# Turning keys by VectorE's block transpose in place of TensorE: half of the cross attention's cached keys, and the first attention's new keys by way of DRAM

## The chip, the cores and the metric

The kernel runs on one core of a Trainium2 chip. The metric is the device time of one execution in microseconds (us). A core has TensorE (PE in the profile, with its weight loads as PEld), VectorE (DVE), ScalarE (ACT), GpSimd (POOL) and SyncE (SP), which here issues the DMAs. Each engine works through its own list of instructions in order, and engines wait for each other by semaphores.

## What is computed

The reference is one step of a streaming encoder of two layers, width 1024, in float32. There are 640 rows: a prompt of 512 frames, and 16 new frames of each of 8 running streams, which have 256 cached frames.

```python
for i in range(DEPTH):                    # 2 layers
    h = rmsnorm(x, g_mix[i])
    o = fox_mixer(h) if i % 2 == 0 else mla_mixer(h)
    x = x + o
    x = x + cross_attn(rmsnorm(x, g_cross[i]), mem_k[i], mem_v[i], w_x_q[i], w_x_o[i])
    x = x + swiglu(rmsnorm(x, g_ffn[i]), w_ffn_gu[i], w_ffn_down[i])

def fox_mixer(h, past):                   # 16 heads of 64
    q, k, v, f_pre, gate = split(h @ w_in)
    k_all = concat([past_k, k])           # k (640 x 1024) is an output too
    s = q @ k_all.T * scale + cumulative log forget bias   # causal
    return (softmax(s) @ v_all * sigmoid(gate)) @ w_out

def cross_attn(h, mk, mv, w_q, w_o):      # 4 heads of 256, 256 memory rows
    q = h @ w_q
    s = q @ mk.T * scale                  # mk: 8 cached streams, 1 prompt
    return (softmax(s) @ mv) @ w_o
```

Scores are sums over the head's dimension, so TensorE wants the keys with that dimension on the partitions. In memory they stand the other way round, a frame to a row, and have to be turned.

## The kernel before

The phases run one after the other: `fox_phase`, `cross_phase(0)`, the feed-forward, the MLA attention, `cross_phase(1)`, the feed-forward. Operands are split into a high and a low part (`whi`/`wlo` of a weight, `hT`, `qT`, `kT` of activations, two buffers each), and a product is three passes of matmuls over them (`PASSES`). `load_w` loads a weight in units of 128 x 1024 elements: a DMA into `raw`, a cast by ACT to `whi` (L150), a subtraction by DVE to `wlo` (L151). The projections' matmuls stand at L204.

`merge` takes lists of steps and interleaves them evenly. A scheduler then fixes from these steps the order of instructions of each engine, so an edit of one list can move the instructions of others. PE works in order, and a matmul that waits holds up all behind it; SP issues nearly all DMAs, in order too.

**The first attention.** Two heads make a pair `pr` (0 to 7), two pairs a group `g` (0 to 3). `k_list(g)` computes 256 columns of new keys, row by row, into `krow` (640 rows as 5 tiles), stores them as outputs, and `tr(j)` turns them for each pair: four PE transposes of the prompt's rows (L539), one of the streams' rows (L543), then `kT` (high by ACT, low by DVE, L222/L223) and `kn` (L544). The cached keys `kr` are brought in pieces of 32 features (L684) and turned by DVE's block transpose (L692). For each pair, `prompt_list(pr)` computes the prompt's attention in three rounds: scores of query tile 3 (L627, 512 columns, 6 matmuls for two heads), the softmax (a reduction by DVE, L634; an exponential by ACT, L637; reciprocal and scaling by DVE, L344 and L345), transposes of the weights on PE (L650) with their copies to `PT` (L655 by DVE, L657 by ACT), then tile 2 (384 columns), their values (L665), and tiles 1 and 0. `sample_list(pr)` does the streams' part (scores L712 with `Qbd` and `KT`). What fills PE between the steps of this chain is `fill`: the projections of the next pair (`q_list`, `k_list`, `v_list`) and the output projection of the pair before.

**The cross attention.** For each of two pairs of heads, two halves of the streams, two heads and four streams, `keys(hh, b)` turns one block of cached keys (256 rows x 256 features) of `kr`: four PE transposes (L956), then one copy to `KT`, by DVE for even `b` (L960), by ACT for odd (L962). There are 32 blocks in a layer, 64 in all. The queries `q_list(h)` take their weights from `w_x_q`.

Of the kernel before, what the change touches and what calls it, by code (L numbers as in the profile page):

```python
# [9 lines left out]
F32 = mybir.dt.float32  # L10
F32R = mybir.dt.float32r
# [7 lines left out]
P = 128  # L19
D = 1024  # L20
KD = D // P
NP = 512
NT = 640
# [69 lines left out]
def fox_mla_kernel(ctx: ExitStack, tc: tile.TileContext, I, O):  # L93
# [42 lines left out]
    def psum_t():  # L136
        return pat.tile([P, 512], F32, tag="t", name="ps_t", bufs=2)
# [267 lines left out]
    def fox_phase():  # L405
# [8 lines left out]
        with ExitStack() as st:  # L414
# [5 lines left out]
            ckd = drp.tile([NH, NP], F32, name="ckd")  # L420
            csd = drp.tile([P, KS], F32, name="csd")
            lfd = drp.tile([P, NH], F32, name="lfd")
            Qbd = [fp.tile([P, B, 32], F32, name=f"Qbd{i}", bufs=1) for i in range(2)]

            def pw_tile():
# [96 lines left out]
            def k_list(g):  # L522
                c0 = 256 * g
                d = {}

                def load():
                    d["w"] = load_w([(0, 256, w_in[:, 1024 + c0:1024 + c0 + 256])])
                    d["row"] = fp.tile([P, TT, 256], F32, tag="krow", name="krow", bufs=1)

                def store():  # L530
                    S.dma_start(ko[:, :, c0:c0 + 256], d["row"][:, 0:TT - 1, :])
                    S.dma_start(kso[:, c0:c0 + 256], d["row"][:, TT - 1, :])

                def tr(j):
                    cs_ = slice(j * P, (j + 1) * P)
# [6 lines left out]
                    pt = psum_t()  # L542
                    T.transpose(out=pt[:, 0:P], in_=d["row"][:, TT - 1, cs_], identity=ident)  # L543
                    V.tensor_copy(kn, pt[:, 0:P])  # L544
                    ks[2 * g + j] = (kT, kn)

                L = [load]
                for t in range(TT):
                    L += gemm(lambda t=t: as_ops(nx.T, slice(t * P, (t + 1) * P), d["w"], slice(0, 256), KD), 256,
                              lambda ps, t=t: A.copy(d["row"][:, t, :], ps[:, 0:256]), parts=2)  # L550
                return L + [store, lambda: tr(0), lambda: tr(1)]

            def q_list(pr):
                c0 = P * pr
# [236 lines left out]
                    nx.all(t + 1)  # L791
                vl[1 + t]()
            vl[-1]()
            merge(logf_list(), k_list(0) + q_list(0))
            mems = mem_list(0, lambda: fp) + mem_list(1, lambda: fp)
            for pr in range(8):
                fill = []
                if pr % 2 == 1 and pr < 7:
                    fill += k_list(pr // 2 + 1)
# [28 lines left out]

    def cross_phase(l, nx, rest):
        w_q, w_o = I["w_x_q"][l], I["w_x_o"][l]  # L830
        mk = I["cache_mem_k"][l].rearrange("b (m p) h d -> p (b m) (h d)", p=P)
        mv = I["cache_mem_v"][l].rearrange("b (m p) h d -> p (b m) (h d)", p=P)
        with tc.tile_pool(name=f"x{l}", bufs=2, reuse_waits="tile") as xp:
            AHEAD = 3
# [5 lines left out]
            def q_list(h):  # L840
                Q = Qps[h // 2]
                L = []
                d = {}

                def load(dt):
                    if dt == 0:
                        qs_[h] = [xp.tile([P, 2, NP], F32R, tag=f"qT{i}", name=f"qT{i}", bufs=2) for i in range(2)]
                    c0 = h * XD + dt * P
                    d[dt] = load_w([(0, P, w_q[:, c0:c0 + P])], per=8)

                def done(ps, dt, half):
                    qT = qs_[h]
                    n = HALF if half == 0 else NP - HALF
                    hs = slice(half * HALF, half * HALF + n)
                    evac_split(qT[0][:, dt, hs], qT[1][:, dt, hs], ps[:, 0:n], X_SCALE)
                    if half == 1:
                        o = TS * (h % 2)
                        A.activation(Q[:, 2 * (h % 2) + dt, :, o:o + TS],
                                     ps[:, n:HALF].rearrange("p (b t) -> p b t", t=TS), AF.Copy, scale=X_SCALE)

                for half in range(2):
                    for dt in range(2):
                        if half == 0:
                            L.append(lambda dt=dt: load(dt))
                        L += gemm(lambda dt=dt, half=half: ws_ops(d[dt], slice(0, P), nx.T,
                                                                  slice(half * HALF, (half + 1) * HALF), KD),
                                  HALF, lambda ps, dt=dt, half=half: done(ps, dt, half), parts=3)
                return L

            def softmax(pw, sp):  # L870
                nm = small.tile([P, 1], F32, tag="nm", name="nm")
# [5 lines left out]
            def prompt_list(h):  # L877
# [57 lines left out]
            def load_key(n):  # L935

                if n < 32:
                    pr, bq, hh, b = n // 16, n // 8 % 2, n // 4 % 2, n % 4
                    hc = slice((2 * pr + hh) * XD, (2 * pr + hh + 1) * XD)
                    krs[n] = xp.tile([P, 2, XD], F32, tag="kr", name="kr", bufs=4)  # L940
                    S.dma_start(krs[n], mk[:, 2 * (4 * bq + b):2 * (4 * bq + b) + 2, hc])

            def sample_list(pr, bq):
                Q = Qps[pr]
# [2 lines left out]
                def keys(hh, b):  # L947
                    n = 16 * pr + 8 * bq + 4 * hh + b
                    load_key(n + AHEAD)
                    kr = krs.pop(n)  # L950
                    if b % 2 == 0:
                        d["KT"][hh, b // 2] = xp.tile([P, 2, 2, NMEM], F32, tag="KT", name="KT", bufs=4)
                    pt = psum_t()
                    for dt in range(2):
                        for mt in range(2):
                            T.transpose(out=pt[:, dt * NMEM + mt * P:dt * NMEM + (mt + 1) * P],  # L956
                                        in_=kr[:, mt, dt * P:(dt + 1) * P], identity=ident)
                    src = pt.rearrange("p (d m) -> p d m", m=NMEM)
# [71 lines left out]
            for n in range(AHEAD):  # L1030
                load_key(n)
            ql = q_list(0)
            for f in ql[:6] + rest[:1] + ql[6:8] + rest[1:] + ql[8:] + q_list(1):
# [761 lines left out]
```

## Time and profile before

| | before |
|---|---|
| median of 3 runs | 2091.75 us (2089.7 to 2093.53) |
| the profiled execution's own time | 2091.71 us |
| its span, first to last instruction | 2089.9 us |
| PE busy | 2034.7 us, 97% |
| DVE busy | 1390.8 us, 67% |
| ACT busy | 888.0 us, 42% |
| granted TensorE clock, mean | 0.996 |
| DMA, mean share of 16 engines | 38.8% |

The time outside the span is 1.8 us. Busy times of matmuls overlap each other, because they are pipelined: a single one shows longer than the distance from its start to the next one's. What a matmul costs PE is therefore read from starts.

### The profile page before, as it was taken

What the parts mean: (1) busy time and instruction counts of PE and PEld (TensorE: products, weight loads), DVE (VectorE), ACT (ScalarE), POOL (GpSimd) and SP (SyncE); (2) the same over time, 40 slices, a digit from 0 to 9 for tenths busy, and PEclk for the clock granted to TensorE, in tenths of its full rate; (3) what the DMA queues carried; (4) which work ended last, traced back from release to release, by engine and by line L of the source; (5) the groups of instructions that cost most, each with busy time, mean ns of one, the idle gap of its engine ahead of it and who ended that gap; (6) DMA issues with size and microseconds to landing.
All of it is one profiled execution on the core that took longest, in us unless ns stands there. A gap on an engine that the chain in (4) does not pass through costs nothing. (4 is left out here: it accounts for less than half of the span.)

```text
span 2089.9 us, 34810 instructions
## 1 busy us (share of the span) xinstructions
PE 2034.7 (97%) x13629; PEld 1817.9 (87%) x13629; DVE 1390.8 (67%) x2658; ACT 888.0 (42%) x1723; POOL 195.2 (9%) x398
## 2 busy tenths in 40 slices
PE   7999999999999999999999989999999999999998
PEld 7988888777987899999998978887987899999996
DVE  5455555655556896687677567777556896686686
ACT  4434444544443443343344455554443443343342
POOL 1222222210000000000002301101000000000000
PEclk9999999999999999999999999999999999999999
DMA  7565655477464322232222342113463322232221
GB/s 194 119 160 124 148 135 142 146 243 229 151 197 133 100 88 74 81 91 71 81 82 64 96 109 52 53 51 102 149 196 131 101 81 75 80 99 71 81 81 61
DMA packets 334203, 236.37 MB, mean 113 GB/s; under 512 B 99140, under 2 KB 298564, under 8 KB 334040
## 3 DMA queue, kind: packets, MB, share of 16 engines
q1 hardware_dynamic: 334040, 234.15, 38.8%
q8 instruction: 108, 1.77, 0.4%
q14 instruction: 55, 0.45, 0.1%
HBM read 216.90 MB, written 17.21 MB: 112 GB/s over the span
## 5 line engine op out<-in xcount | busy, mean ns | idle before, releaser
L204 PE MATMUL mm<-hT,whi 128*128 128x320 f32 x1744 | 287.5, 311 | 2.9 <-ACT hT L222 2.9
L151 DVE TENSOR_TENSOR wlo<-raw,whi 128x1024 fp32r<-128x1024 f32 (+4 forms) x145 | 169.8, 1174 | 156.5 <-ACT whi L150 116.5
L204 PEld LDWEIGHTS mm<-hT,whi 128*128 128x128 f32 x1744 | 261.0, 188 | 6.8 <-ACT hT L222 4.3
L332 DVE TENSOR_TENSOR X<-mm,X 128x512 f32<-128x512 f32 x270 | 183.5, 687 | 119.7 <-PE mm L204 118.1
L150 ACT CAST whi<-raw 128x1024 fp32r<-128x1024 f32 (+4 forms) x145 | 144.8, 1003 | 146.7 <-PE mm L204 74.9
L204 PE MATMUL mm<-whi,oT 128*128 128x512 f32 x544 | 180.3, 407 | 3.8 <-DVE X L332 2.2
L1136 ACT CAST whi<-tw 128x512 fp32r<-128x512 f32 (+1 forms) x120 | 91.9, 766 | 213.7 <-PE mm L204 127.4
L204 PE MATMUL mm<-whi,aT 128*128 128x512 f32 x560 | 173.0, 390 | 1.2 <-ACT aT L1101 1.2
L204 PE MATMUL mm<-hT,wlo 128*128 128x320 f32 x872 | 156.7, 312 | 0.0
L204 PEld LDWEIGHTS mm<-hT,wlo 128*128 128x128 f32 x872 | 133.3, 188 | 3.3 <-issue 3.2
L232 POOL TENSOR_SCALAR rstd<-ss 128x1 f32<-128x1 f32 x49 | 16.2, 330 | 1265.4 <-ACT hn L230 1261.0
L204 PE MATMUL mm<-s,whi 128*128 128x320 f32 x768 | 128.2, 309 | 0.0
L204 PE MATMUL mm<-whi,hT 128*128 128x256 f32 (+2 forms) x800 | 125.5, 295 | 0.3 <-ACT whi L150 0.3
L204 PEld LDWEIGHTS mm<-whi,aT 128*128 128x128 f32 x560 | 104.4, 188 | 23.5 <-ACT aT L1101 2.0
L204 PEld LDWEIGHTS mm<-whi,oT 128*128 128x128 f32 x544 | 96.7, 189 | 26.2 <-DVE X L332 4.6
L204 PEld LDWEIGHTS mm<-s,whi 128*128 128x128 f32 x768 | 116.6, 188 | 0.0
L1137 DVE TENSOR_TENSOR wlo<-tw,whi 128x512 fp32r<-128x512 f32 (+1 forms) x120 | 103.5, 862 | 19.1 <-ACT whi L1136 17.4
L204 PEld LDWEIGHTS mm<-whi,hT 128*128 128x128 f32 x800 | 109.1, 191 | 3.8 <-issue 1.7
L204 PE MATMUL mm<-wlo,oT 128*128 128x512 f32 x272 | 109.0, 401 | 0.0
L204 PE MATMUL mm<-wlo,aT 128*128 128x512 f32 x280 | 108.8, 389 | 0.0
L1136 ACT CAST whi<-raw 128x1024 fp32r<-128x1024 f32 x44 | 46.3, 1052 | 131.7 <-PE mm L204 71.0
L204 PE MATMUL ps_s<-whi,aT 128*128 128x512 f32 x320 | 98.6, 389 | 0.0
(336 smaller groups left out, 4199.4 us busy)
## 6 DMA issues: line engine op xcount, KB each, us to landing
rawg<-w_ffn_gu SPq DMA_DIRECT2D x80, 512.0 KB, 3.8
raw<-w_ffn_down SPq DMA_DIRECT2D x44, 512.0 KB, 3.7
raw<-w_x_kv SPq DMA_DIRECT2D x32, 512.0 KB, 4.4
kr<-cache_mem_k SPq DMA_DIRECT2D x64, 256.0 KB, 4.8
vr<-cache_mem_v SPq DMA_DIRECT2D x32, 512.0 KB, 6.1
raw<-w_fox_in SPq DMA_DIRECT2D x30, 512.0 KB, 6.5
kr<-cache_fox_k SPq DMA_DIRECT2D x64, 128.0 KB, 5.1
vr<-cache_fox_v SPq DMA_DIRECT2D x16, 512.0 KB, 5.2
```

The costliest lines, as they stand in the source:

```text
L150: A.copy(hi[:, 0:m], raw[:, 0:m])
L151: V.tensor_tensor(lo[:, 0:m], raw[:, 0:m], hi[:, 0:m].bitcast(F32), ALU.subtract)
L204: T.matmul(st["ps"][:, 0:n], lhsT=l, rhs=r, start=(j == 0), stop=(j == m - 1))
L232: G.tensor_scalar(r, ss, EPS, None, ALU.add)
L332: V.tensor_tensor(xs, ps, xs, ALU.add)
L1136: A.copy(hi[:, o:o + m], src)
L1137: V.tensor_tensor(lo[:, o:o + m], src, hi[:, o:o + m].bitcast(F32), ALU.subtract)
```

## The change

**Cross attention.** The blocks with even `b` (32 of 64) are loaded by four DMAs instead of one, each with 64 features of 32 rows to a partition (pieces of 256 bytes; 1 KB before), and turned by one DVE transpose straight to `KT`. Their four PE transposes and the copy are gone. A 32 x 32 block transpose leaves the features in another order (features of one parity on each half), so all that meets these keys takes the same order: the queries' weights, the odd blocks and the prompt's keys are read with a stride of two elements as PE's stationary operand. `w_x_q` is loaded as two units of 256 columns for both parities.

**First attention.** `krow` is stored once more, to a DRAM tile `kd[g]` (640 KB), and read back by `back(j)` in four DMAs for a pair, in pieces of 128 bytes, to `kraw`. Two DVE transposes make `kt` (prompt) and `kn` (streams) of it; `kT` is split from `kt`. Their five PE transposes and the copy of `kn` are gone, for all 8 pairs. The two `tr` steps are taken out of `k_list`'s list and stand at the end of the fill.

The diff, cut to its core:

```diff
+            kd = [drp.tile([NT, 256], F32, name=f"kd{g}") for g in range(4)]
...
                 def store():
+                    S.dma_start(kd[g].rearrange("(t p) n -> p t n", p=P), d["row"])
...
+                def back(j):
+                    r = d["raw", j] = fp.tile([P, NT // 32, 32], F32, tag="mrow", name="kraw", bufs=2)
+                    src = kd[g].rearrange("(m j) n -> j m n", j=32)
+                    for i in range(4):
+                        o = j * P + 32 * i
+                        S.dma_start(r[32 * i:32 * i + 32], src[:, :, o:o + 32])
...
                 def tr(j):
-                    pt = psum_t()
-                    for t in range(TT - 1):
-                        T.transpose(out=pt[:, t * P:(t + 1) * P], in_=d["row"][:, t, cs_], identity=ident)
-                    evac_split(kT[0], kT[1], pt)
...
-                    T.transpose(out=pt[:, 0:P], in_=d["row"][:, TT - 1, cs_], identity=ident)
-                    V.tensor_copy(kn, pt[:, 0:P])
+                    kt = fp.tile([P, NP], F32, tag="pw", name="kt", bufs=4)
+                    V.transpose(kt, d["raw", j][:, 0:NP // 32].rearrange("p m x -> p (m x)"))
+                    V.transpose(kn, d["raw", j][:, NP // 32:].rearrange("p m x -> p (m x)"))
+                    evac_split(kT[0], kT[1], kt)
...
-                return L + [store, lambda: tr(0), lambda: tr(1)]
+                return L + [store, lambda: back(0), lambda: back(1)], [lambda: tr(0), lambda: tr(1)]
...
-            merge(logf_list(), k_list(0) + q_list(0))
+            kl, kt = k_list(0)
+            merge(logf_list(), kl + q_list(0) + kt)
...
                 if pr % 2 == 1 and pr < 7:
                     fill += q_list(pr + 1)
+                fill += kt
...
+                    hs = slice(half * HALF, (half + 1) * HALF)
+                    return [(d["w"].get(wi, k).rearrange("p (n t) -> p t n", t=2)[:, dt], nx.T[ai][:, k, hs])
+                            for wi, ai in PASSES for k in range(KD)]
...
+            def fill_keys(r, src, h):
+                for g in range(4):
+                    c0 = h * XD + 64 * g
+                    S.dma_start(r[32 * g:32 * g + 32], src[:, :, c0:c0 + 64])
+
+            def turn_keys(dst, r):
+                V.transpose(dst, r.rearrange("p m (i t) -> p t m i", t=2))
...
-                                        in_=d["kv"][0][:, mt, dt * P:(dt + 1) * P], identity=ident)
+                                        in_=d["kv"][0][:, mt].rearrange("p (n t) -> p t n", t=2)[:, dt], identity=ident)
...
                     if b % 2 == 0:
                         d["KT"][hh, b // 2] = xp.tile([P, 2, 2, NMEM], F32, tag="KT", name="KT", bufs=4)
+                        turn_keys(d["KT"][hh, b // 2][:, 0], kr)
+                        return
...
-                                        in_=kr[:, mt, dt * P:(dt + 1) * P], identity=ident)
...
-                    if b % 2 == 0:
-                        V.tensor_copy(d["KT"][hh, b // 2][:, 0], src)
-                    else:
-                        A.copy(d["KT"][hh, b // 2][:, 1], src)
+                                        in_=kr[:, mt].rearrange("p (n t) -> p t n", t=2)[:, dt], identity=ident)
+                    A.copy(d["KT"][hh, b // 2][:, 1], pt.rearrange("p (d m) -> p d m", m=NMEM))
```

**The order.** On PE, at the scores and transposes of pair 0, the rows before are these. L627 are the scores of query tile 3 (512 columns), L650 the transposes of their softmax, L204 matmuls of the projections.

```order
L627 MATMUL ps_s<-kT_537,qT_589 128x512 x2
L627 MATMUL ps_s<-kT_538,qT_589 128x512 x2
L627 MATMUL ps_s<-kT_537,qT_590 128x512 x2
L204 MATMUL mm<-hT_139,whi 128x320 x4
L204 MATMUL mm<-hT_140,whi 128x320 x4
L204 MATMUL mm<-hT_141,whi 128x320 x4
L204 MATMUL mm<-hT_142,whi 128x320 x4
L204 MATMUL mm<-hT_139,wlo 128x320 x4
L204 MATMUL mm<-hT_140,wlo 128x320 x4
L650 MATMUL ps_t<-cst,pw 128x128 x8
```

The same place with the change, where the scores' line is L633, the transposes' L656, the streams' scores L718 and the values L671.

```order
L633 MATMUL ps_s<-kT_714,qT_558 128x512 x2
L204 MATMUL mm<-hT_143,wlo 128x320 x2
L633 MATMUL ps_s<-kT_715,qT_558 128x512 x2
L633 MATMUL ps_s<-kT_714,qT_559 128x512 x2
L204 MATMUL mm<-hT_143,wlo 128x320 x2
L204 MATMUL mm<-hT_144,wlo 128x320 x4
L633 MATMUL ps_s<-kT_714,qT_558 128x384
L633 MATMUL ps_s<-kT_715,qT_558 128x384
L633 MATMUL ps_s<-kT_714,qT_559 128x384
L633 MATMUL ps_s<-kT_714,qT_558 128x384
L656 MATMUL ps_t<-cst,pw 128x128 x4
```

Between the scores of tile 3 and their transposes stood 24 matmuls of projections; now 6 stand there behind the last of the scores, and four scores of tile 2.

On DVE, at the same place with the change: L226 makes `qT` of pair 1 from a projection, L548 and L549 are the new transposes (`kraw` was read back from DRAM), L223 the low part of `kT`, L640 the softmax's reduction.

```order
L226 SCALAR_TENSOR_TENSOR qT_737<-mm,qT_736 128x320
L548 STREAM_TRANSPOSE kt<-kraw 128x512
L549 STREAM_TRANSPOSE kn<-kraw 128x128
L223 TENSOR_TENSOR kT_715<-kt,kT_714 128x512
L226 SCALAR_TENSOR_TENSOR qT_737<-mm,qT_736 128x192
L548 STREAM_TRANSPOSE kt<-kraw 128x512
L549 STREAM_TRANSPOSE kn<-kraw 128x128
L223 TENSOR_TENSOR kT_723<-kt,kT_722 128x512
L640 ISA pw,nm<-ps_s,pw 128x512
```

Before, `kT` of both pairs was done some ten rows earlier, and one L226 stood right ahead of the reduction; now a second L226, the turned keys of pair 1 and their low part stand between the scores' keys and the reduction of these scores.

On PE, at pair 2, the rows before:

```order
L627 MATMUL ps_s<-kT_1510,qT_1674 128x512 x2
L627 MATMUL ps_s<-kT_1511,qT_1674 128x512 x2
L627 MATMUL ps_s<-kT_1510,qT_1675 128x512 x2
L204 MATMUL mm<-hT_139,wlo 128x320 x4
L204 MATMUL mm<-hT_140,wlo 128x320 x4
L204 MATMUL mm<-hT_139,whi 128x320 x4
L204 MATMUL mm<-hT_140,whi 128x320 x4
L204 MATMUL mm<-hT_141,whi 128x320 x4
L204 MATMUL mm<-hT_142,whi 128x320 x4
L204 MATMUL mm<-hT_139,wlo 128x320 x4
L204 MATMUL mm<-hT_140,wlo 128x320 x4
L650 MATMUL ps_t<-cst,pw 128x128 x8
```

And with the change:

```order
L633 MATMUL ps_s<-kT_1933,qT_1648 128x512 x2
L633 MATMUL ps_s<-kT_1934,qT_1648 128x512 x2
L633 MATMUL ps_s<-kT_1933,qT_1649 128x512 x2
L204 MATMUL mm<-hT_143,wlo 128x320 x4
L204 MATMUL mm<-hT_144,wlo 128x320 x4
L633 MATMUL ps_s<-kT_1933,qT_1648 128x384 x2
L633 MATMUL ps_s<-kT_1934,qT_1648 128x384 x2
L633 MATMUL ps_s<-kT_1933,qT_1649 128x384 x2
L656 MATMUL ps_t<-cst,pw 128x128 x4
L718 MATMUL ps_s<-KT,Qbd_100 32x272 x4
L656 MATMUL ps_t<-cst,pw 128x128 x7
L671 MATMUL ps_o<-PT,vsb 64x128
```

Of 32 matmuls of projections between scores and transposes, 8 are left; from the scores of tile 2 to the values no projection stands between. Pair 4 has the same rows as pair 2. At pair 6 the scores of tiles 3 and 2 follow each other directly, then the streams' scores and eight transposes. At the odd pairs, the cross attention's other steps and the other phases the pattern of rows stays.

## Rows read from the trace of the kernel before

**Rows 1.** The page, engines' busy time, share, instructions.

```profile
PE 2034.7 (97%) x13629; PEld 1817.9 (87%) x13629; DVE 1390.8 (67%) x2658; ACT 888.0 (42%) x1723; POOL 195.2 (9%) x398
```

**Rows 2.** Windows: stretch, length, busy time by engine, granted clock, DMA share, GB/s.

```profile
45.00:115.00 70.00, 68.51 (x580) 63.96 (x580) 30.39 (x77) 28.76 (x62) 16.65 (x35) 1.00 0.64 153
...
560.00:680.00 120.00, 119.57 (x953) 100.24 (x951) 68.18 (x141) 49.04 (x113) 0.00 (x0) 1.00 0.52 169
```

**Rows 3.** Waits of PE: us in total, times, longest.

```profile
PE ps_t L543 <- ACT krow L550: 1.1, 1, 1.1
...
PE ps_t L956 <- DMA kr<-cache_mem_k: 0.8, 3, 0.4
```

**Rows 4.** Instructions on tile kr: duration in ns, min/median/max, starts, forms.

```profile
L956 PE MATMUL ps_t<-cst,kr x256: 270/272/330, 557.8 to 1605.4; 128*128 128x128 f32 x128
...
L692 DVE STREAM_TRANSPOSE KT<-kr x32: 669/696/712, 36.6 to 398.5; 128x512 f32<-128x512 f32 x32
```

**Rows 5.** Timeline of PE in the first cross attention: start, duration.

```profile
568.78 0.60 PE L956 MATMUL ps_t<-cst,kr 128*128 128x128 f32 x4
569.14 1.41 PE L204 MATMUL mm<-hT,wlo 128*128 128x320 f32 x8
570.38 1.60 PE L218 MATMUL ps_o<-PT,v 128*128 128x256 f32 x12
```

**Rows 6.** Timeline of PE at the turning of krow.

```profile
50.77 0.61 PE L539 MATMUL ps_t<-cst,krow 128*128 128x128 f32 x4
51.21 0.27 PE L543 MATMUL ps_t<-cst,krow 128*128 128x128 f32 x1
51.24 0.54 PE L204 MATMUL mm<-hT,whi 128*128 128x320 f32 x2
```

**Rows 7.** Timeline of PE, projections alone.

```profile
57.88 1.34 PE L204 MATMUL mm<-hT,wlo 128*128 128x320 f32 x8
59.05 1.19 PE L204 MATMUL mm<-hT,whi 128*128 128x320 f32 x7
```

**Rows 8.** Weight loads by line and form: count, busy us, mean ns, idle before.

```profile
L204 PEld LDWEIGHTS mm<-hT,whi 128*128 128x128 f32 x1744 | 261.0, 188 | 6.8 <-ACT hT L222 4.3 <-DVE KT L692 1.3 <-ACT qT L225 0.4
...
L956 PEld LDWEIGHTS ps_t<-cst,kr 128*128 128x128 f32 x256 | 30.0, 140 | 6.1 <-DMA kr<-cache_mem_k 2.2 <-ACT KT L962 1.6 <-DVE KT L960 0.4
...
L969 PEld LDWEIGHTS ps_s<-KT,Qp 128*32 128x32 f32 x256 | 7.5, 109 | 6.3 <-issue 1.1 <-ACT hn L874 0.7 <-ACT qT L225 0.4
```

**Rows 9.** Timeline of PE at pair 0, scores to transposes.

```profile
70.38 0.96 PE L627 MATMUL ps_s<-kT,qT 64*128 64x512 f32 x6
71.27 2.61 PE L204 MATMUL mm<-hT,whi 128*128 128x320 f32 x16
73.72 1.34 PE L204 MATMUL mm<-hT,wlo 128*128 128x320 f32 x8
74.90 1.03 PE L650 MATMUL ps_t<-cst,pw 128*128 128x128 f32 x8
```

**Rows 10.** Timeline of DVE at the same place.

```profile
71.50 0.69 DVE L634 CUSTOM_DVE_ANT_0 pw<-ps_s,pw 128x512 f32<-128x512 f32 x1
...
72.72 1.22 DVE L151 TENSOR_TENSOR wlo<-raw,whi 128x1024 fp32r<-128x1024 f32 x1
...
74.06 0.88 DVE L345 TENSOR_SCALAR pw<-pw,rc 128x512 f32<-128x512 f32 x2
...
76.26 0.68 DVE L655 COPY PT<-ps_t 128x512 f32<-128x512 f32 x1
```

**Rows 11.** Timeline of ACT at the same place.

```profile
72.23 0.72 ACT L637 ACTIVATE pw<-pw,nm 128x512 f32<-128x512 f32 x1 [0.37 <-DVE nm L634]
```

**Rows 12.** The page, DMA issues: KB each, median us from issue to landing.

```profile
kr<-cache_mem_k SPq DMA_DIRECT2D x64, 256.0 KB, 4.8
...
kr<-cache_fox_k SPq DMA_DIRECT2D x64, 128.0 KB, 5.1
```

**Rows 13.** Timeline of SP's queue: the last store of krow.

```profile
49.11 0.36 SPq L532 DMA_DIRECT2D out_fox_k_s<-krow  x1
```

More of the change, by code (lines that the diff above doesn't have):

```diff
@@ L530, in store @@
                 def store():
+                    S.dma_start(kd[g].rearrange("(t p) n -> p t n", p=P), d["row"])
                     S.dma_start(ko[:, :, c0:c0 + 256], d["row"][:, 0:TT - 1, :])
                     S.dma_start(kso[:, c0:c0 + 256], d["row"][:, TT - 1, :])
+                def back(j):
[4 more added lines that the diff above has]
+                        S.dma_start(r[32 * i:32 * i + 32], src[:, :, o:o + 32])
                 def tr(j):
-                    cs_ = slice(j * P, (j + 1) * P)
                     kT = [fp.tile([P, NP], F32R, tag=f"kT{i}", name=f"kT{i}", bufs=3) for i in range(2)]
-                    pt = psum_t()
-                    for t in range(TT - 1):
-                        T.transpose(out=pt[:, t * P:(t + 1) * P], in_=d["row"][:, t, cs_], identity=ident)
-                    evac_split(kT[0], kT[1], pt)
                     kn = fp.tile([P, P], F32, tag="kn", name="kn", bufs=3)
-                    pt = psum_t()
-                    T.transpose(out=pt[:, 0:P], in_=d["row"][:, TT - 1, cs_], identity=ident)
-                    V.tensor_copy(kn, pt[:, 0:P])
+                    kt = fp.tile([P, NP], F32, tag="pw", name="kt", bufs=4)
+                    V.transpose(kt, d["raw", j][:, 0:NP // 32].rearrange("p m x -> p (m x)"))
+                    V.transpose(kn, d["raw", j][:, NP // 32:].rearrange("p m x -> p (m x)"))
+                    evac_split(kT[0], kT[1], kt)
                     ks[2 * g + j] = (kT, kn)
@@ L793, in fox_phase @@
             vl[-1]()
-            merge(logf_list(), k_list(0) + q_list(0))
+            kl, kt = k_list(0)
+            merge(logf_list(), kl + q_list(0) + kt)
             mems = mem_list(0, lambda: fp) + mem_list(1, lambda: fp)
             for pr in range(8):
-                fill = []
+                fill, kt = [], []
                 if pr % 2 == 1 and pr < 7:
-                    fill += k_list(pr // 2 + 1)
+                    kl, kt = k_list(pr // 2 + 1)
+                    fill += kl
                 elif pr < 7:
@@ L830, in cross_phase @@
         w_q, w_o = I["w_x_q"][l], I["w_x_o"][l]
-        mk = I["cache_mem_k"][l].rearrange("b (m p) h d -> p (b m) (h d)", p=P)
+        mkp = I["cache_mem_k"][l].rearrange("b (m p) h d -> p (b m) (h d)", p=P)
+        mk = I["cache_mem_k"][l].rearrange("b (m j) h d -> b j m (h d)", j=32)
         mv = I["cache_mem_v"][l].rearrange("b (m p) h d -> p (b m) (h d)", p=P)
@@ L843, in q_list, with load, ops @@
                 d = {}
[L845 to L849, printed above, removed]
+                def load():
+                    qs_[h] = [xp.tile([P, 2, NP], F32R, tag=f"qT{i}", name=f"qT{i}", bufs=2) for i in range(2)]
+                    d["w"] = load_w([(0, XD, w_q[:, h * XD:(h + 1) * XD])])
+                def ops(dt, half):
+                    hs = slice(half * HALF, (half + 1) * HALF)
+                    return [(d["w"].get(wi, k).rearrange("p (n t) -> p t n", t=2)[:, dt], nx.T[ai][:, k, hs])
+                            for wi, ai in PASSES for k in range(KD)]
                 def done(ps, dt, half):
@@ L862, in q_list @@
                     for dt in range(2):
[L863 to L868, printed above, removed]
+                        L += gemm(lambda dt=dt, half=half: ops(dt, half), HALF,
+                                  lambda ps, dt=dt, half=half: done(ps, dt, half), parts=3)
+                return [load] + L
+            def fill_keys(r, src, h):
[4 more added lines that the diff above has]
+                V.transpose(dst, r.rearrange("p m (i t) -> p t m i", t=2))
             def softmax(pw, sp):
@@ L938, in load_key @@
                     pr, bq, hh, b = n // 16, n // 8 % 2, n // 4 % 2, n % 4
-                    hc = slice((2 * pr + hh) * XD, (2 * pr + hh + 1) * XD)
-                    krs[n] = xp.tile([P, 2, XD], F32, tag="kr", name="kr", bufs=4)
-                    S.dma_start(krs[n], mk[:, 2 * (4 * bq + b):2 * (4 * bq + b) + 2, hc])
+                    if b % 2 == 0:
+                        krs[n] = xp.tile([P, 8, 64], F32, tag="kr", name="kr", bufs=4)
+                        fill_keys(krs[n], mk[4 * bq + b], 2 * pr + hh)
+                    else:
+                        hc = slice((2 * pr + hh) * XD, (2 * pr + hh + 1) * XD)
+                        krs[n] = xp.tile([P, 2, XD], F32, tag="kr", name="kr", bufs=4)
+                        S.dma_start(krs[n], mkp[:, 2 * (4 * bq + b):2 * (4 * bq + b) + 2, hc])
             def sample_list(pr, bq):
@@ L956, in keys @@
                             T.transpose(out=pt[:, dt * NMEM + mt * P:dt * NMEM + (mt + 1) * P],
-                                        in_=kr[:, mt, dt * P:(dt + 1) * P], identity=ident)
-                    src = pt.rearrange("p (d m) -> p d m", m=NMEM)
-                    if b % 2 == 0:
-                        V.tensor_copy(d["KT"][hh, b // 2][:, 0], src)
-                    else:
-                        A.copy(d["KT"][hh, b // 2][:, 1], src)
+                                        in_=kr[:, mt].rearrange("p (n t) -> p t n", t=2)[:, dt], identity=ident)
+                    A.copy(d["KT"][hh, b // 2][:, 1], pt.rearrange("p (d m) -> p d m", m=NMEM))
                 def scores():
@@ L1032, in cross_phase @@
             ql = q_list(0)
-            for f in ql[:6] + rest[:1] + ql[6:8] + rest[1:] + ql[8:] + q_list(1):
+            for f in ql[:5] + rest[:1] + ql[5:7] + rest[1:] + ql[7:] + q_list(1):
                 f()
```

## Prediction

> **What bounds the kernel now.** The page's busy times come first: PE is busy 97% of the span, DVE 67% [rows 1]. Time is saved where PE has fewer columns to pass or stops waiting, and lost where PE waits for others; the question is whether either happens where the change works. The windows by stage answer for the two places. In the first attention (45 to 115 us) PE has 68.5 of 70 us and DVE 30.4; in the cross attention (560 to 680) PE has 119.6 of 120, DVE 68.2 [rows 2]. So both stages are PE's, and DVE has room for a transposition in place of a copy. PE's waits at the edited lines are small: 1.1 us for `krow` and 0.8 us for cached keys [rows 3]. The whole of the gain must then come from PE's own work, and a loss from waits that are not there yet. Those I looked for in the new order of instructions, timed with the durations of the old trace.
>
> The profiled execution took 2091.71 us with its 1.8 us outside the span, 0.04 under the median of the runs, so the sum is made against 2091.7.
>
> **What goes away: cross attention.** A group of four transposes on keys takes 270 ns each by the tile's rows [rows 4], but these overlap. By starts, PE goes from 568.78 to 569.14, 0.36 us for four; the eight projection matmuls behind them take 1.24 us from start to start, where eight elsewhere take 59.05 - 57.88 = 1.17 [rows 5, 7]. With this, a group costs PE 0.43 to 0.44 us. 32 blocks lose theirs: 32 x 0.44 = **-14.1 us**. On DVE the copy of 128 x 512 (0.68 us for the same shape [rows 10]) gives way to a transpose of 128 x 512 at 0.696 us [rows 4]: 32 x 0.02 = 0.6 us more, under PE's cover. The transposes of the first attention read runs of elements, the new ones read every second; if that doubled them, DVE would have 16 x 0.7 = 11 us more in a layer's cross attention, of which the stage has about 50 us idle in 120 [rows 2].
>
> **What goes away: first attention.** Five transposes stand between 50.77 and 51.24: 0.47 us, and with the same 0.07 behind them 0.54 [rows 6]. Eight such groups: **-4.3 us**. The 1.1 us wait for `krow` goes with them, and of the 0.8 us for cached keys half: **-1.5 us** [rows 3].
>
> **What is added at nothing, and its price otherwise.**
> - *Stride on PE.* 768 projection matmuls of `w_x_q` (two layers, 4 heads, 96 each) and 160 transposes (128 of odd blocks, 32 of the prompt's keys) read their stationary operand at every second element. No row of before has such a load. Plain loads take 188 ns at 128 columns and 109 at 32 [rows 8], that is (188 - 109) / 96 = 0.82 ns a column, 105 for 128, beneath a pitch of 1.17 / 8 = 146 ns [rows 7]. If stride costs less than 40 ns a load, all is hidden: 0. If it doubled the columns' time, 210 - 146 = 64 ns would show 768 times: **+49 us**, and for the transposes, whose pitch is 90 ns [rows 5] and whose load is 140 [rows 8], 17 to 57 ns x 160 = 3 to 9 us. I take 0, since elements of two neighbouring columns stand only 8 bytes apart; both ends stay in the range of cases below.
>
> The Trainium skill, page "SBUF — State Buffer", section "Door 1: The DMA port swizzle (why `[64,N]` ≈ `[32,N]`)", says that SBUF is read in lines of 16 bytes and that two hits in a line are enough to cover the access. Stride two on float32 makes just two hits, so by this rule the price is 0; every third element would not have been free. No run here shows it so far.
>
> - *DMA.* Cached keys now come in pieces of 256 bytes. The nearest row is the first attention's `kr`: pieces of 128 bytes, 5.1 us from issue to landing, against 4.8 us for pieces of 1 KB [rows 12]. Keys are loaded three blocks ahead, about 3 x 3.7 us of a stage of 120 us with 32 blocks, so 5 to 6 us is in time. Price 0; if each of 32 came 1 us late, 32 us, but a landing above 11 us has no row.
>
> The Trainium skill's page "DMA: Bandwidth & Descriptors", section "Specifications", speaks against this: it wants 512 bytes in a transfer for full rate. The rows' 5.1 us at 128 bytes against 4.8 us at 1 KB, for half the bytes, agree in the direction; by the page the added pieces would load the queues to a fuller share, which the 0.52 of rows 2 leaves room for.
>
> - *Through DRAM.* The last store of `krow` was issued at 49.1 us [rows 13]. One landing for the store (about 5 us [rows 12]), the issue of eight reads behind it (0.4 us each, 3 us), and one landing of those reads: 49.1 + 5 + 3 + 5 = 62 us, an estimate. The scores of pair 0 start at 70.4 [rows 9], and would at about 68.6 with what is saved ahead of them. Seven us of slack: 0. While SP waits for the store, weights and `kr` are queued behind it for some 5 to 8 us in each of four groups; two `raw` buffers and three of `whi`/`wlo` stand ahead of PE, about as long. Nothing is late by this account, but barely.
>
> **What is moved: the new waits.** This is the term that decides. At pair 0, 24 projection matmuls stood between the scores of tile 3 and their transposes: 71.27 to 74.90, 3.6 us [rows 9]. Under them ran the softmax: reduction at 71.50 (0.69), exponential at 72.23 (0.72), scaling at 74.06 (0.88 for two heads), after a `wlo` of 1.22 [rows 10, 11]. Without that `wlo` the chain needs from the end of the scores 0.2 + 0.7 + 0.7 + 0.2 (reciprocal) + 0.45 + a handover of 0.1 = 2.4 us for the first head; then the transposes of 0.36, a copy to `PT` of 0.7 with its handovers, and the values.
>
> - *Pair 0, new order.* Behind the scores come 6 projections (0.9 us), four scores of tile 2 and then the transposes. And DVE reaches the reduction only after the second L226 (which needs those 6 projections), a transpose of 128 x 512, one of 128 x 128 and a low part: 0.35 + 0.7 + 0.25 + 0.7 = 2.0 us, after ACT's 0.35 for the high part. The first transposes can start some 0.1 + 0.35 + 2.0 + 2.2 = 4.7 us behind the projections, PE comes after 0.5: it waits over 4. My replay of all rows of PE, DVE and ACT by these durations gives 4.8 us there and 3.9 in what follows (second head, tile 2, values): **+8.7 us**.
> - *Pairs 2 and 4.* Eight projections (1.17) and the scores of tile 2 (0.7) stand ahead of the first transposes: 1.9 us against 2.4 to 2.65, a wait of 0.5 to 0.8. From there to the values nothing but the chain's own work is left, and DVE has it one after the other: four reductions, four scalings, four reciprocals, two `PT` copies and a `qT`, 5.7 us at the rows' durations. The rows of PE up to its next projection are 5.6 us of work; the replay ends after 10.7: **+5.1 us** for each pair. If DVE never idled, it would still be about 8.8: +3.2.
> - *Pair 6.* Here the streams' scores stand in between: **+2.7 us** by the replay.
>
> Sum 8.7 + 5.1 + 5.1 + 2.7 = **+21.6 us**; the lower bound, with DVE never idle in pairs 2 and 4 and only the first wait and half of the rest at the others, is 6.4 + 6 + 1.5 = 14, the upper, with a handover of 0.2 more at some 25 steps, 27. I take the replay, which uses measured distances throughout. The odd pairs keep their projections between. In the cross attention eight places between the streams' scores and their transposes lose filler, 1.7 us where about 1.9 is needed: 8 x 0.2 = **+1.6 us**.
>
> **Sum.** -14.1 - 4.3 - 1.5 + 21.6 + 1.6 = +3.3: 2091.7 + 3.3 = **2095 us**. The gain of the cross attention is eaten by the first attention's new order. Its own range is 2088 to 2101, by the bounds of the waits.
>
> **The rivals.**
> - *Faster: the chains overlap better.* The waits at a pair are not added up but run into each other: while PE waits for one head, DVE and ACT finish the other, so only half of the replayed wait shows. For it: DVE has more than half of the stage idle [rows 2], and the scheduler's order may have placed rows where they are ready. Against: DVE's list is serial and has 5.7 us at pairs 2 and 4 alone. At 11 us: 2091.7 - 18.3 + 11 = 2084. It decides below waits of 14 us.
> - *Stride shows.* Doubled loads: 2095 + 49 + 6 = 2150; only the transposes: 2098 to 2104. For the first: the load already takes 188 of its pipelined time [rows 8]; against: 40 ns of room at a matmul.
> - *The way through DRAM is late.* Pair 0's keys come after 70 us, or the weights queued behind SP's wait do. The point is a delay of 7 us; for 8 us of delay beyond, 2103. For it: SP is in order, and the DMA share is already 0.64 here [rows 2].
>
> **How the numbers follow.** Forecast 0.45, faster rival 0.26, stride 0.15 (0.07 doubled, 0.08 small), DRAM 0.14. Within 0.2% (about what a measurement here can tell from no change) is 2087.6 to 2095.9. Faster has the rival and 0.04 of the forecast: 0.30. Same has half of the forecast, its sum lying near the edge, and some of the small cases: 0.29. Slower has the rest: 0.41. The range 2080 to 2112 leaves out the doubled stride, and 0.06 on either side.
>
> **What would show it.** Right: the block transposes of `kr` on DVE near 0.7 us, 256 PE transposes at the key's line become 128, the cross stages each 6 to 7 us shorter, and in the first attention PE waits for DVE's and ACT's softmax (`pw`, `PT`) at pairs 0, 2, 4 and 6, some 20 us in all, which the table of waits doesn't have now. Wrong: no such waits (then about 2073), projections of `w_x_q` at a pitch above 150 ns, or PE waiting for `kT` at pair 0.

## The result, and the profile after

The change made the kernel slower: 2105.95 us median (2100.57 to 2107.99, 5 runs) against 2092.36 of before (2089.7 to 2095.58, 5 runs). The ratio is 1.0062, with an interval of 1.0044 to 1.008; the forecast of 2095 us lay 11 us below.

The page of the changed kernel, its busy times, and then the main waits of PE that are new or longer (us in total, times, longest):

```profile
PE 2031.5 (96%) x13461; PEld 1814.0 (86%) x13461; DVE 1396.0 (66%) x2666; ACT 883.4 (42%) x1723; POOL 189.0 (9%) x398
```

```profile
...
PE ps_s L633 <- DVE nm L640: 6.5, 4, 4.0
PE mm L388 <- ACT whi L150: 4.5, 4, 1.9
...
PE ps_t L246 <- DVE hn L238: 3.7, 2, 3.1
...
PE ps_t L656 <- DVE pw L345: 2.3, 5, 0.8
```

PE is busy 3 us less than before [rows 1], though some 18 us of its work are gone by the forecast's count (14.1 + 4.3), and the span is 15.6 us longer: PE waits more, and part of the work that is left runs slower. The waits behind the softmax are there (L633, L656), as forecast; those for `whi` at L388, the matmuls of `mem_list` (the cross attention's prompt keys and values, computed in the fill of pairs 6 and 7), were not.

Where the time went is read from windows that begin with the scores of a pair's tile 3. The last two rows are pair 7 up to the first projection of the cross attention, and all that follows. Columns as in [rows 2]. First the changed kernel (pairs 0, 2, 4, 6, 7, rest):

```profile
70.60:126.20 55.60, 50.80 (x405) 42.39 (x404) 24.73 (x66) 20.56 (x47) 16.43 (x33) 0.91 0.56 139
...
171.30:229.30 58.00, 54.59 (x435) 47.59 (x434) 30.44 (x75) 21.58 (x48) 12.51 (x27) 0.94 0.55 139
275.10:330.50 55.40, 53.69 (x435) 46.82 (x434) 29.83 (x75) 21.59 (x48) 11.55 (x24) 0.97 0.59 149
377.50:451.60 74.10, 67.68 (x395) 52.38 (x394) 43.09 (x86) 33.58 (x61) 16.46 (x29) 0.95 0.64 188
451.60:557.60 106.00, 90.65 (x498) 69.84 (x497) 59.63 (x101) 51.58 (x85) 14.46 (x30) 0.98 0.66 213
557.60:2105.00 1547.40, 1515.62 (x9738) 1374.98 (x9738) 1094.00 (x1989) 649.70 (x1250) 80.80 (x163) 1.00 0.34 98
```

The same stretches of the kernel before:

```profile
70.40:116.80 46.40, 45.99 (x423) 42.35 (x422) 22.92 (x63) 21.19 (x48) 12.30 (x24) 1.00 0.62 141
...
164.80:218.00 53.20, 51.94 (x435) 45.38 (x434) 28.11 (x73) 20.27 (x46) 11.58 (x24) 1.00 0.57 132
266.00:320.10 54.10, 52.01 (x437) 45.38 (x436) 28.16 (x72) 21.18 (x48) 12.53 (x26) 1.00 0.62 149
370.70:439.10 68.40, 67.15 (x411) 52.58 (x410) 42.07 (x85) 33.84 (x62) 15.10 (x28) 1.00 0.56 181
439.10:527.30 88.20, 82.66 (x474) 65.02 (x473) 53.67 (x94) 46.28 (x79) 14.11 (x27) 0.98 0.69 224
527.30:2089.00 1561.70, 1529.74 (x9866) 1385.47 (x9866) 1094.80 (x1990) 652.93 (x1250) 80.15 (x163) 1.00 0.32 96
```

Three things stand in these rows. The cross attention begins 557.6 - 527.3 = 30.3 us later, and everything behind it takes 14 us less (1561.7 - 1547.4). At pairs 0, 2, 4 and 6 PE idles (length less busy time) 16.3 us where it idled 5.0, and the granted clock is below 1.00, where it was 1.00. And pair 7, where the order of instructions has no thin place, takes 17.8 us more, 9.8 of it idle, with 24 more matmuls (498 against 474). The even pairs take 21.0 us more in all (243.1 against 222.1), pairs 1, 3 and 5 by the same windows 8.7 less; with pair 7 that is 30.1 of the 30.3.

What the low clock is, PE's timeline at pair 0 shows:

```profile
72.16 1.15 PE L204 MATMUL mm<-hT,wlo 128*128 128x320 f32 x6
77.33 0.78 PE L633 MATMUL ps_s<-kT,qT 64*128 64x384 f32 x3 [4.03 <-DVE nm L640]
...
79.57 1.11 PE L656 MATMUL ps_t<-cst,pw 128*128 128x128 f32 x4
```

PE waits 4.03 us for the reduction, and behind that wait four transposes go from 79.57 to 80.62, 1.05 us, where four took 0.36 [rows 5]. In stretches of 5 us the clock is 0.50 from 80 to 85 us, the lower of its two levels. Four transposes take nearly three times as long, so the halved clock isn't all of it.

### The profile page after: what moved, and what is told of

Same layout as the page of the kernel before. It is cut to its first block, busy times and chain, and to the rows that moved or that the text cites. A ratio compares the mean times of both kernels' runs of the same rounds, so it can differ in the third digit from the quotient of the medians.

```text
span 2105.5 us, 34587 instructions
## 1 busy us (share of the span) xinstructions
PE 2031.5 (96%) x13461; PEld 1814.0 (86%) x13461; DVE 1396.0 (66%) x2666; ACT 883.4 (42%) x1723; POOL 189.0 (9%) x398
## 5 line engine op out<-in xcount | busy, mean ns | idle before, releaser
L204 PE MATMUL mm<-hT,whi 128*128 128x320 f32 x1744 | 293.1, 314 | 3.8 <-ACT hT L222 3.8
L204 PEld LDWEIGHTS mm<-hT,whi 128*128 128x128 f32 x1744 | 263.8, 191 | 12.7 <-ACT hT L222 5.2
L204 PE MATMUL mm<-whi,oT 128*128 128x512 f32 x544 | 176.8, 403 | 5.0 <-DVE X L332 2.8
L204 PE MATMUL mm<-whi,aT 128*128 128x512 f32 x560 | 173.0, 390 | 0.4 <-ACT aT L1123 0.4
L204 PE MATMUL mm<-hT,wlo 128*128 128x320 f32 x872 | 154.8, 312 | 0.0
L204 PEld LDWEIGHTS mm<-hT,wlo 128*128 128x128 f32 x872 | 133.5, 190 | 3.8 <-issue 3.8
L204 PE MATMUL mm<-s,whi 128*128 128x320 f32 x768 | 128.2, 309 | 0.0
L204 PE MATMUL mm<-whi,hT 128*128 128x256 f32 (+2 forms) x800 | 125.5, 296 | 0.1
L204 PEld LDWEIGHTS mm<-whi,aT 128*128 128x128 f32 x560 | 104.4, 188 | 22.7 <-ACT aT L1123 1.2
L204 PEld LDWEIGHTS mm<-whi,oT 128*128 128x128 f32 x544 | 98.4, 189 | 26.6 <-DVE X L332 4.2
L204 PEld LDWEIGHTS mm<-s,whi 128*128 128x128 f32 x768 | 116.6, 188 | 0.0
L204 PEld LDWEIGHTS mm<-whi,hT 128*128 128x128 f32 x800 | 109.4, 192 | 2.9 <-issue 1.1
L204 PE MATMUL mm<-wlo,aT 128*128 128x512 f32 x280 | 108.8, 389 | 0.0
L204 PE MATMUL mm<-wlo,oT 128*128 128x512 f32 x272 | 107.9, 398 | 0.0
L204 PE MATMUL ps_s<-whi,aT 128*128 128x512 f32 x320 | 98.6, 389 | 0.0
```

The source lines that it names most:

```text
L204: T.matmul(st["ps"][:, 0:n], lhsT=l, rhs=r, start=(j == 0), stop=(j == m - 1))
```

## The experiments

Each ratio is to the kernel before, timed beside the run.

**The halves alone.** `cross_alone` has the new `cross_phase` and the old `fox_phase`; `fox_alone` the other way round.

> The cross attention's half of the change alone; the first attention is as before. Theory A (the two halves add up; in the changed kernel everything behind the start of the cross attention's projections is 14.7 us shorter): 2092 - 14 = 2078 us, and the projections of w_x_q keep a start-to-start distance of 146 to 148 ns a matmul. Theory B (strided stationary loads or the smaller DMA pieces cost something that the sum hides): 2085 us or more.

> The first attention's half alone; the cross attention is as before. Theory A (the halves add up): 2092 + 28 = 2120 us, with the granted clock at half speed for some 10 us after pairs 0, 2, 4 and 6's scores. Theory B (the late end of the first attention, pair 7, comes of the cross attention's loads that follow it): 2110 us, with pair 7 as long as before.

`cross_alone` 2078.56 against 2094.06, ratio 0.9922 (0.9906 to 0.9939); `fox_alone` 2118.57, ratio 1.0111 (1.0095 to 1.0127). The halves add up within their intervals: -15.5 and +24.5 make +9, where the whole change measured +13.6. So the loss is the first attention's, and it is larger than the forecast's +16.2 for it (21.6 - 4.3 - 1.1).

The strided reads, in the changed kernel (weight loads of the cross attention's projections from 557.6 to 587 us; then the transposes of keys; then PE's timeline of projections):

```profile
L204 PEld LDWEIGHTS mm<-hT,whi 128*128 128x128 f32 x128 | 19.1, 196 | 2.4 <-ACT hT L222 2.4
```

```profile
L982 PEld LDWEIGHTS ps_t<-cst,kr x128: 194/207/223, 588.0 to 1623.2; 128*128 128x128 f32 x128
```

```profile
577.56 2.51 PE L204 MATMUL mm<-hT,whi 128*128 128x320 f32 x16
579.91 1.34 PE L204 MATMUL mm<-hT,wlo 128*128 128x320 f32 x8
```

A strided load takes 196 ns where a plain one takes 188, and a transpose's 207 where it took 140 [rows 8]. Sixteen projections go from 577.56 to 579.91, 147 ns each, as before [rows 7]: hidden. Four transposes take 0.38 to 0.40 us instead of 0.36: 160 x 8 ns = 1.3 us in all.

**Where the keys are turned, and when.** `pe_turn_end` is the changed kernel with TensorE's transposes out of `krow` and no way through DRAM; it differs from `cross_alone` only in that the two steps stand at the end of the fill.

```diff
-                return L + [store, lambda: back(0), lambda: back(1)], [lambda: tr(0), lambda: tr(1)]
+                return L + [store], [lambda: tr(0), lambda: tr(1)]      # tr as in the kernel before, no kd
```

> As the changed kernel, but the new keys are turned by TensorE out of krow as before, with the two steps left at the end of the fill, and no way through DRAM. Theory A (the way through DRAM sets the thin order at pairs 0, 2, 4 and 6): projections stand between scores and transposes again, no low clock there, and 2079 us, as the cross attention's half alone. Theory B (the place of the two steps in the list does it): the waits and the low clock stay, 2095 us or more.

2071.6 us, ratio 0.9888 (0.9872 to 0.9904): no low clock at pairs 0 to 6, and the fastest kernel of this study. The moved steps are not the trouble; they are worth 7 us (2078.56 - 2071.6), which I had not forecast. So the way through DRAM, VectorE's turning included, costs 2106 - 2071.6 = 34 us.

**Useless work in the gaps.** `busy_pe` fills the waits at pairs 0, 2 and 4.

```diff
                         pt = psum_t()
+                        if pr in (0, 2, 4) and qts != [1, 0]:
+                            for _ in range(10 if pr == 0 and qts == [3] and hh == 0 else 3):
+                                T.matmul(pt, lhsT=nx.T[0][:, 0, 0:P], rhs=nx.T[0][:, 0, 0:512], start=True, stop=True)
```

> The changed kernel with useless work added: 43 matmuls of 512 columns (10 us at their distance of 0.23 us) in front of the transposes of pairs 0, 2 and 4, where TensorE waits; their results are overwritten. Theory A (the idle time lets the granted clock fall, and the low clock costs another 5.0, 3.5 and 1.7 us at these pairs): the clock stays at 1.00 there, and the time falls by 7 to 10 us, to 2096 to 2099 us, in spite of the added work. Theory B (only the waits themselves cost): the added work fills waits or lengthens them, 2106 to 2112 us.

2105.3 us: no change. Pairs 0, 2 and 4 of this run (and the stretch of pair 7):

```profile
70.80:126.90 56.10, 54.03 (x423) 45.84 (x423) 24.59 (x66) 20.55 (x47) 16.44 (x33) 0.94 0.55 137
...
171.90:228.60 56.70, 55.36 (x447) 47.84 (x446) 31.25 (x75) 21.68 (x48) 12.34 (x27) 1.00 0.55 140
274.40:329.70 55.30, 55.09 (x449) 47.86 (x448) 30.95 (x75) 21.67 (x48) 12.94 (x28) 1.00 0.61 151
...
450.40:556.20 105.80, 91.95 (x498) 71.05 (x497) 59.40 (x101) 51.71 (x85) 14.78 (x29) 0.97 0.66 212
```

At pairs 2 and 4, with 12 added matmuls each, the clock is 1.00 now; at pair 0, with 19, it still falls (0.94, where it was 0.91). Pair 0 is 0.5 us longer, pairs 2 and 4 are 1.3 and 0.1 us shorter, and the end of the first attention moves by 1.4. Theory A's 7 to 10 us didn't come. But the run doesn't price the low clock either: over the three pairs PE idles 6.3 us less and is busy 5.4 us more, so the added work (43 x 0.23 = 10 us) filled the idle time and used up what the clock gave back.

**The DMAs without their use.** `dma_only` is `pe_turn_end` with the store to `kd` and the eight reads a group, which nothing uses. `reads_free` is `dma_only` without the store; its reads take a part of `w_fox_in`, and wait for nothing.

```diff
                 def store():
+                    S.dma_start(kd[g].rearrange("(t p) n -> p t n", p=P), d["row"])     # dma_only
...
-                    src = kd[g].rearrange("(m j) n -> j m n", j=32)
+                    src = w_in[0:NT, 0:256].rearrange("(m j) n -> j m n", j=32)          # reads_free
```

> The run pe_turn_end (2071.6 us) with the way through DRAM added and not used: krow is stored to kd and read back in eight DMAs a group, nothing reads kraw, TensorE turns the keys out of krow as before. The order of instructions already shows thin places at pairs 2, 4 and 6 (8 projections between scores and transposes), none so thin at pair 0. Theory A (the DMAs on SP's queue alone push weights and cached keys back, and with them the projections that filled the chain): low granted clock and waits at pairs 2, 4 and 6, the loads of w_x_kv as late as in the changed kernel, 2092 to 2100 us. Theory B (VectorE's turning, which comes after the read-back, makes the loss): 2072 to 2077 us.

> The run dma_only (2106.7 us) without the store to kd: the eight reads a group, of the same size and pieces and on the same queue, take a part of w_fox_in instead and wait for no store; nothing uses them. Theory A (the reads' wait for the store's landing, with SP's queue and then the order behind it, makes the loss): projections stand between scores and transposes at every pair but one, no low clock at pairs 0 to 5, 2072 to 2082 us. Theory B (the number of small DMAs on SP's queue and the DMA engines' load make it): 2095 us or more.

`dma_only`: 2106.72, ratio 1.0058 (1.0043 to 1.0073), as slow as the changed kernel and past theory A's 2100. VectorE's turning in place of TensorE's neither costs nor saves anything that can be seen; the DMAs make the whole loss. `reads_free`: 2098.86, ratio 1.0022 (1.001 to 1.0034), 27 us over `pe_turn_end`. Its even pairs are as short as there (221.0 us against 221.7) and its clock is 1.00 at pairs 2 to 6; pairs 1, 3 and 5 take 10.5 us more, with a clock of 0.94 at pair 1, and pair 7 takes 17.6 more. So most of the loss needs neither the wait for the store nor thin places at the even pairs. Theory A's price falls; what is left is theory B's: the number of DMAs on SP's queue, or the load of the DMA engines.

**The keys a pair earlier, and in other buffers.** `k_early` gives the chain its projections back with the way through DRAM kept; `kt_own` takes `kt` out of the softmax's buffers.

```diff
+                if pr % 2 == 0 and pr < 6:
+                    kl, kts = k_list(pr // 2 + 1)      # k_early: k_list with even pairs, v_list with odd
+                    fill += kl
...
-                    kt = fp.tile([P, NP], F32, tag="pw", name="kt", bufs=4)
+                    kt = npool.tile([P, D], F32, tag="hn", name="hn", bufs=2)[:, 0:NP]      # kt_own
```

> The changed kernel with the new keys of a group computed a pair earlier: k_list in the fill of the even pairs, v_list in that of the odd ones, the two turning steps in the odd pair's fill ahead of q_list. The turning is VectorE's, by way of DRAM, as in the changed kernel; the order shows 12 or more projections behind the scores at every pair. Theory A (the thin order makes the loss, not the way through DRAM as such): clock 1.00 at pairs 0 to 6, 2068 to 2078 us. Theory B (contention of the added DMAs, or VectorE's longer list, makes it): 2090 us or more.

> The changed kernel with kt in buffers of its own rather than in those of the softmax's pw, with the same order of TensorE's scores. Theory A (a small part: at pair 0 the reduction waits for POOL's bias in a pw buffer that kt held): 2103 to 2105 us, pair 0 shorter by 1 to 2 us. Theory B (the shared buffers are the main cause): 2085 us or less. Theory C: no difference.

`kt_own`: 2105.55, no difference. `k_early`: 2099.58, ratio 1.0028 (1.0018 to 1.0037), by its time theory B's, though from pair 1 on the clock is theory A's. From pair 1 to pair 7 it takes 309.3 us, less than the 315.6 of `pe_turn_end`, at a clock of 1.00; but its pair 0 has 57.4 us, and its pair 7 has 112.0 where `pe_turn_end` has 87.2. So the thin order explains what happens at the pairs ahead, and pair 7 is something else: it begins 14.5 us earlier than in the changed kernel (437.1 against 451.6) and ends only 8.5 earlier.

**SP's queue ahead of pair 7.** What pair 7 waits for are the weights of `mem_list`, 32 loads `w_x_kv`. The idle time of PE before the matmuls of L388 that `whi` ended (us, times), in the changed kernel and in the one before:

```profile
  ACT whi L150: 11.1, 9
...
  ACT whi L150: 0.4, 1
```

It is 0.4 us in `cross_alone` and nothing in `pe_turn_end`, but 9.1 in `dma_only`, 13.1 in `reads_free` and 7.0 in `k_early`. ACT, which makes `whi`, waits in turn for the loads to land, over pair 7 of the changed kernel and of the one before:

```profile
ACT whi L150 <- DMA raw<-w_x_kv: 24.6, 11, 6.0
...
ACT whi L150 <- DMA raw<-w_x_kv: 8.7, 8, 2.0
```

SP's timeline in the changed kernel ahead of the first of these loads:

```profile
341.81 7.20 SPq L542 DMA_DIRECT2D kraw<-kd  x8
349.05 1.15 SPq L690 DMA_DIRECT2D kr<-cache_fox_k  x2
366.02 0.39 SPq L692 DMA_DIRECT2D vr<-cache_fox_v  x1
366.45 2.59 SPq L608 DMA_DIRECT2D ckb<-ckd  x2
369.08 3.93 SPq L690 DMA_DIRECT2D kr<-cache_fox_k  x4
373.12 0.86 SPq L692 DMA_DIRECT2D vr<-cache_fox_v  x1
374.08 0.82 SPq L148 DMA_DIRECT2D raw<-w_fox_in  x1
374.99 1.27 SPq L148 DMA_DIRECT2D raw<-w_fox_out  x1
...
386.75 1.51 SPq L148 DMA_DIRECT2D raw<-w_x_kv  x2
```

And what SP waited for from 345 to 390 us:

```profile
SPq L692 <- PE ps_o L746: 15.7, 1, 15.7
```

In the kernel before:

```profile
344.77 0.33 SPq L148 DMA_DIRECT2D raw<-w_fox_out  x1
...
353.49 0.39 SPq L148 DMA_DIRECT2D raw<-w_x_kv  x1
...
355.74 1.35 SPq L686 DMA_DIRECT2D vr<-cache_fox_v  x2
```

Before, the last weights of the first attention and the first `w_x_kv` stood ahead of the cached values `vr`; with the added DMAs the order of the queue has `vr` ahead. `vr` waits until PE has used its buffer in the pair before, 15.7 us, and those weights stand behind it: 386.75 instead of 353.49. Of these 33.3 us, 10.3 are that `vr` itself is late (366.02 against 355.74); the rest is the place in the queue, where the first load stood 2.3 us ahead of `vr` and now stands 20.7 behind it. From its first load to its last the stream of 32 takes about the same time in all kernels of the table, 135 to 144 us (here 353.5 to 495.9 and 386.8 to 525.7), and so the first projection of the cross attention follows the first load by a nearly fixed distance. Both were read from SP's and PE's timelines:

| kernel | first `w_x_kv` load, us | first cross projection, us | distance |
|---|---|---|---|
| before | 353.5 | 527.3 | 173.8 |
| `cross_alone` | 353.8 | 527.8 | 174.0 |
| `pe_turn_end` | 345.3 | 519.6 | 174.3 |
| `reads_free` | 375.4 | 546.9 | 171.5 |
| `k_early` | 380.2 | 549.1 | 168.9 |
| changed | 386.8 | 557.6 | 170.8 |
| `busy_pe` | 385.9 | 556.2 | 170.3 |
| `dma_only` | 386.8 | 556.8 | 170.0 |

In the first three, without added DMAs, the first load stands ahead of `vr`; in the other five behind it. Its start, moved by +33.3 us in the changed kernel, fits the +30.3 us, and it fits that filling the gaps won nothing and that `k_early` lost in pair 7 what it had won ahead. `fox_alone` and `kt_own` have 170.6 and 170.8 us. It is no law: `trip_pool` and `both_pool` below have 189.3 and 193.5.

The DMA engines' load remains as a rival. Their mean share from pair 0's scores to the first cross projection is alike, 0.61 against 0.60 before and 0.61 in `pe_turn_end`; but a `w_x_kv` load lands after 5.6 us, where it took 4.4 before (medians).

**Other queues.** `trip_pool` issues store and reads from GpSimd, `all_dve` turns all cached cross keys by VectorE (on `pe_turn_end`), `all_dve_pool` does that with GpSimd's DMAs, `both_pool` joins `trip_pool` and `all_dve_pool`.

```diff
-                        S.dma_start(r[32 * i:32 * i + 32], src[:, :, o:o + 32])
+                        G.dma_start(r[32 * i:32 * i + 32], src[:, :, o:o + 32])     # trip_pool; kd's store too
...
-                    S.dma_start(r[32 * g:32 * g + 32], src[:, :, c0:c0 + 64])
+                    G.dma_start(r[32 * g:32 * g + 32], src[:, :, c0:c0 + 64])       # all_dve_pool
```

> The changed kernel with the store to kd and the reads back issued by GpSimd instead of SyncE, and nothing else. The order shows 24 and more projections behind the scores again at pairs 0, 2 and 4, and the loads of w_x_kv stand as early as before. Theory A (the place in SP's queue makes the whole loss): no low clock at pairs 0 to 6; the 4.3 us of TensorE's transposes come off the run pe_turn_end: 2066 to 2072 us. Theory B (the way through DRAM costs as such: DMA engines, or the late keys): 2085 us or more. A further cost may come from GpSimd issuing DMAs while it prepares the softmax's bias.

> The run pe_turn_end (2071.6 us) with all 64 blocks of cached cross keys turned by VectorE, so 128 more transposes of TensorE are gone, and ACT's copies too. Theory A (the cross stages stay TensorE's): another 32 x 0.44 = 14 us, 2058 us. Theory B (VectorE is late with the turned keys, or the smaller DMA pieces are, now 32 blocks in a row): 2066 us or more, with waits of TensorE on KT.

> The run all_dve (2144 us) with the 256 small loads of cached cross keys issued by GpSimd instead of SyncE. Theory A (its 72 us over pe_turn_end came of SP's queue, where the loads hold up weights): 2057 to 2066 us, clock 1.00 in the cross attention. Theory B (VectorE with 64 transposes is late, or the small pieces are): 2100 us or more.

> The first attention of trip_pool and the cross attention of all_dve_pool together: no key is turned by TensorE except the prompt's cross keys. Theory A: the gains add, 2052 to 2062 us, faster than any of these kernels. Theory B: as the slower of the two.

All four were slower than the kernel before, against every theory A: 2141.21 (1.0223, 1.0199 to 1.0247), 2144.05 (1.0241, 1.0226 to 1.0256), 2127.91 (1.0157, 1.0133 to 1.0181) and 2204.49 (1.052, 1.0498 to 1.0542). GpSimd's timeline in `trip_pool`:

```profile
58.82 0.69 POOL L542 DMA_DIRECT2D kraw<-kd  x1 [3.92 <-issue]
61.77 0.69 POOL L542 DMA_DIRECT2D kraw<-kd  x1 [2.26 <-issue]
...
82.08 0.69 POOL L542 DMA_DIRECT2D kraw<-kd  x1 [4.51 <-issue]
82.76 0.42 POOL L694 COPY KT<-kn 128x64 f32<-128x64 f32 x2
```

A read costs GpSimd 3 to 6 us from start to start; the last of eight is issued at 82.08, and the softmax's bias stands behind it. This run put a longer queue in the place of SP's and so says nothing on theory A. For `all_dve`, the stretch from 521 to 741 us:

```profile
521.00:741.00 220.00, 192.23 (x1213) 157.11 (x1213) 123.77 (x217) 68.67 (x147) 7.61 (x14) 0.91 0.49 131
```

VectorE is busy 56%, not the bound; SP issues most of the layer's 128 loads of keys there, four to a block. That its 72 us come of SP's queue fits, but `all_dve_pool`, 16 us faster with the loads on GpSimd's queue, doesn't show it.

## Why the prediction was right in sign and off in size

- **Cross attention, -14.1 + 1.6.** Right: 14 us behind the first projection, -15.5 by `cross_alone`. The 1.6 us of waits weren't looked for by themselves.
- **Stride, 0.** Right for the projections, 1.3 us for the transposes. The rule on lines of 16 bytes (the Trainium skill, "SBUF — State Buffer", section "Door 1: The DMA port swizzle (why `[64,N]` ≈ `[32,N]`)") agrees with the projections' time; it does not with the load itself, 207 ns against 140.
- **VectorE's transposes, hidden.** Right: `dma_only`, which has none of the new ones in the first attention, is as slow, and those of the cross attention, which read every second element, take 702 ns against 696 [rows 4].
- **Smaller pieces of cached cross keys, 0.** Right: the loads of 64 KB land after 3.4 us (median), and VectorE waited 0.7 us for them in all.
- **The steps at the end of the fill.** I took them for the cause of the thin order. `pe_turn_end` shows a gain of 7 us; its mechanism is not settled, though its stream starts 8.5 us earlier than that of `cross_alone`.
- **The waits at pairs 0, 2, 4 and 6, +21.6.** They came, in the places forecast, as 16.3 - 5.0 = 11.3 us more idle time; the low clock, not in my sum, took as much again (0.09 x 55.6 + 0.06 x 58.0 + 0.03 x 55.4 + 0.05 x 74.1 = 13.9 us of full speed). That the even pairs grew by 21.0 us, so near the forecast, is in part luck: the forecast had no term for the clock, and its waits were twice as large. Nor would these pairs alone give the time back: `reads_free` has them as short as `pe_turn_end` and is 27 us slower.
- **Through DRAM, "Nothing is late by this account, but barely".** This is the step that failed. I asked only whether the DMAs land in time, which they do (no engine waits for `kraw` to land in the trace), and not in which order SP's queue stands afterwards. The added DMAs put `vr`, with its wait of 15.7 us, ahead of the weights; the stream of `w_x_kv` starts 33 us late, and the end of the first attention moves with it: +30.3 us against the sum's +16.2. The rival of a late way through DRAM named the weights behind SP's wait, at 8 us and 0.14.

That the added DMAs make the loss is shown. That the end of the first attention hangs on the start of this stream is argued: it rests on the waits for `whi` and on the kernels of the table, none of which moved the stream alone; a kernel with `vr` behind the weights and all else the same wasn't tried. Nor is it settled what sets the stream's pace, or what, in the making of the order, moves `vr`.

## What to carry to other kernels

A DMA on an in-order queue can cost more than its bytes and its landing: look for what stands behind it, and where the next long wait of that queue then comes to stand. Before filling gaps on the busiest engine, look for a stream whose start the end of the stage follows; here it was read from the DMA queue's own timeline. Moving transposes from TensorE to VectorE paid for half of the cached keys, which come from DRAM anyway, and failed where the keys needed a trip of their own.

## What was not expected of the hardware

After a wait of 4 us TensorE ran at its lower clock for some 10 us, until about 88 us; useless matmuls in the gaps of pairs 2 and 4 kept it at 1.00, and more of them at pair 0 didn't (0.94). A stationary operand read at every second element made a transpose's weight load 48% longer (207 against 140 ns), and a projection's only 4% (196 against 188). GpSimd took 3 to 6 us to issue one DMA of 32x20 pieces of 128 bytes; SP took 0.9 (7.20 us for eight).
